# GpSimd's part of the state space preparation held until the first cross attention ends, with its zero blocks written once

## The chip, the core and the metric

The kernel runs on one core of one Trainium2 chip. The metric is device time in microseconds (us) of one launch. The core has five engines that each work through a queue of their own in order: TensorE (PE, with its weight loads shown apart as PEld), VectorE (DVE), ScalarE (ACT), GpSimd (POOL) and SyncE (SP, which here only issues transfers). They meet through semaphores, and an engine whose next instruction waits does nothing behind it either.

## What is computed

Two networks follow each other on 256 rows of 1024 numbers, in float32. The first has two layers, each a hybrid mixer followed by a cross attention to a memory of 256 rows. The second has, in layer 0, a feed-forward block, a state space mixer and a second feed-forward block, and in layer 1 the same with a sparse attention in the middle.

```python
for l in range(2):                                  # first_block
    h = h + hybrid_mixer(rms_norm(h, ...), ...)
    h = h + memory_cross_attention(rms_norm(h, ...), mem, ...)
h = rms_norm(h, norm_final)
h = h + 0.5 * swiglu(rmsnorm(h), ...)               # second_block, layer 0: "ffa0"
h = h + s5_mixer(rmsnorm(h), a, log_dt, b, c, ...)  # "mx20"
...
```

The state space mixer needs matrices that depend on its parameters alone: the discretised input matrices `bb_re`, `bb_im`, powers of the diagonal, and products of these with `b` and `c`. The kernel works them out while the first network runs, in eight tiles of eight groups, and stores them in HBM (`stash`), from where the mixer loads them at about 646 us.

## The kernel before

**The main work.** A weight block arrives from HBM as `raw` (halves of 128 x 1024), ACT copies each half to `hi` (line 156) and DVE forms the rest `lo` (line 157). TensorE multiplies in three products per block (`xh,hi`, `xh,lo`, `xl,hi`, or the like, all issued at line 72). There are three `hi` and two `lo` buffers, so DVE can be one block or so ahead of TensorE.

**Side work.** `Net.bg` is called after most groups of matmuls. It keeps an account: `share` times the modelled time of the matmuls issued is owed to a generator `self.side`, and it advances the generator until the debt is paid by the modelled time of the GpSimd instructions that came out (at least 1000 ns a step). A step that yields a true value ends the call. `share` is 0.4 in the first network and 0.7 in the feed-forward blocks.

**The preparation.** `s5_prep` joins `self.side` at the end of the first mixer. It first computes small parameters on DVE and ACT (`prm`, `pw`, `E`), then on GpSimd `bb` (six products, all GpSimd instructions are recorded at line 60), then the eight tiles of `s5_prep_tile`. A tile does, in GpSimd's order: the zeroing of `pcb` and of `pX` twice, the products that fill the two `pX`, the zeroing of a record buffer `pv` (128 x 1024), four products from `pcb` and four sums into `pv`, two stores (`stash<-pv`, the first of this record, the second of one that ACT filled at line 1302), the zeroing of the next `pv` (128 x 512, twice 128 x 4), eighteen small products, and a third store. In between ACT writes `pcb` from PSUM (lines 1279 and 1280), TensorE transposes the two `pX` and multiplies them with `pcb` (PSUM tag `pq`), and DVE copies blocks into the zeroed `pv` (line 1329). `pv` has two buffers, `pcb` and the two `pX` one each.

GpSimd keeps the order in which it is called (`InOrder`). The other engines' queues are put in order by the framework's scheduler when the program is built, and are fixed from then on. GpSimd also computes the reciprocal roots of the norms (`rq`, `rx`, `rf`), which the main work needs.

**Deadline.** `s5_inputs(2)`, called when the third quarter of ffa0's output is done, runs what is left of the generator.

Of the kernel before, what the change touches and what calls it, by code (L numbers as in the profile page):

```python
# [78 lines left out]
class Net:  # L79
    def __init__(self, ctx, tc, T):  # L80
        self.tc, self.nc, self.T = tc, tc.nc, T
        self.G, self.PE = InOrder(tc), Products(tc)
        self.at, self.owed, self.share = 0, 0, 0.4
        pool = lambda name, bufs, **kw: ctx.enter_context(tc.tile_pool(name=name, bufs=bufs, **kw))
        self.cp = pool("consts", 1)
        self.wp = pool("weights", 3)
        self.wk = pool("work", 2)
        self.sm = pool("small", 2)
        self.dr = pool("dram", 1, space=bass.MemoryType.DRAM)
        self.pp = pool("psum", 3, space=PSUM)  # L90
        self.side = iter(())

    def bg(self):

# [752 lines left out]
    def cross(self, l):  # L847
        nc, T = self.nc, self.T
        V, A, PE = nc.vector, nc.scalar, self.PE
        b1 = self.b1  # L850
        mv = self.t("qT", [P, 6, S], pool=b1).rearrange("p a b -> p (a b)")[:, :1024].rearrange("p (t c) -> p t c", t=2)
        x = self.xhat(self.hT, self.gain("norm_xattn", KD * l, KD))

        def mem_v(i):

            p = self.rows2(self.wcols(T["mem_wv"][l], 256 * i, 256), self.xmem)
            for t in range(2):
                A.activation(mv[:, t, 256 * i:256 * i + 256], p[:, t, :], AF.Copy, scale=self.rm[:, t:t + 1])
            self.bg()
            if i == 1 and l == 0:  # L860
                self.mem = self.mem_in(1)
                self.side = chain(self.mem, self.side)

        qT, kT, pr, xs = [], self.mkT, {}, []

        def queries(hp):
            p = self.proj2(self.wcols(T["mem_wq"][l], hp * 256, 256), x)
            q = self.pair(f"L{hp}", pool=b1)
            A.activation(q, p, AF.Copy)
            qT.append(q)  # L870
            self.bg()

        def scores(h):
            p2 = self.ps("pb").rearrange("p (t k) -> p t k", t=2)
            st = self.c("ast", 8, bufs=4)
            s = self.pair(f"sg{h}", pool=b1) if h < 3 else self.t("keT", [P, 512], pool=b1).rearrange("p (i s) -> p i s", i=2)
            for t in range(2):
                p = p2[:, t, :]
                PE.matmul(p, qT[h // 2][:, h % 2, t * P:(t + 1) * P], kT[:, h, :], start=True, stop=True)
            V.tensor_reduce(st[:, 0:2], p2, axis=AX.X, op=MAX)  # L880
            for t in range(2):
                V.tensor_scalar(st[:, 2 + t:3 + t], st[:, t:t + 1], rs_[:, t:t + 1], -1.0, op0=MUL, op1=MUL)
                A.activation(s[:, t, :], p2[:, t, :], AF.Exp, bias=st[:, 2 + t:3 + t], scale=rs_[:, t:t + 1],
                             accum_out=st[:, 4 + t:5 + t])
            V.reciprocal(st[:, 6:8], st[:, 4:6])
            for t in range(2):
                V.tensor_scalar(s[:, t, :], s[:, t, :], st[:, 6 + t:7 + t], None, op0=MUL)
            pr[h] = s

        def values(h):  # L890
            pt = self.ps("pb").rearrange("p (i s) -> p i s", i=2)
            for kt in range(2):
                for t in range(2):
                    PE.transpose(pt[:, kt, t * P:(t + 1) * P], pr[h][:, t, kt * P:(kt + 1) * P], self.ident)
            sT = self.pair("e2", bufs=3)
            A.activation(sT, pt, AF.Copy)
            po = self.ps("po")[:, :S]
            for kt in range(2):
                PE.matmul(po, mv[:, kt, h * P:(h + 1) * P], sT[:, kt, :], start=kt == 0, stop=kt == 1)
            hl = self.pair(f"L{2 + h}", F32R, pool=b1)  # L900
            hl = [hl[:, 0, :], hl[:, 1, :]]
            A.activation(hl[0], po, AF.Copy)  # L902
            V.tensor_tensor(hl[1], po, hl[0].bitcast(F32), op=SUB)
            xs.append(hl)

        mem_v(0)
        queries(0)
        r = self.rpow(self.sumsq(self.hT, KD, "pb"), D, 2, "rx")
        rs_ = self.c("rxs", 2)
        V.tensor_scalar(rs_, r, 1.0 / math.sqrt(128.0), None, op0=MUL)  # L910
        queries(1)
        scores(0)
        scores(1)
        scores(2)
        mem_v(1)
        values(0)
        scores(3)
        values(1)

        ws = [self.wcols(T["mem_wo"][l], c0, 512, nk=4) for c0 in (0, 512)]  # L920
        add = self.add_h()
        bank = {}

        def part(m2, ks):
            if m2 not in bank:
                bank[m2] = self.ps().rearrange("p (i s) -> p i s", i=2)
            for k in ks:
                for i in range(2):
                    c = (2 * (m2 % 2) + i) * P
                    self.mm3(bank[m2][:, i, :], [w_[:, k, c:c + P] for w_ in ws[m2 // 2]], xs[k], k + i == 0, k == 3,  # L930
                             skip_group_check=True)

        part(0, (0, 1))
        values(2)
        part(1, (0, 1))
        values(3)
        part(2, (0, 1))
        for m2 in range(4):
            part(m2, (2, 3) if m2 < 3 else range(4))
            add(m2, bank[m2])  # L940
            self.bg()

    def first_block(self):
        nc, T = self.nc, self.T
# [186 lines left out]
    def s5_prep(self):  # L1131
# [63 lines left out]
        for k in range(6):  # L1195
# [3 lines left out]
            if k == 3:  # L1199
# [17 lines left out]
        TT(v["zi"], v["zi"], v["dt"], MUL)  # L1217
        yield

        bb = self.pz.tile([P, 2, 512], F32, name="bb", tag="bb", bufs=1)  # L1220
        GT = lambda o, a, b, op: G.tensor_tensor(o, a, b, op=op)
        zb = [v[n][:, :, None].to_broadcast([P, H, 16]) for n in ("zr", "zi")]
# [2 lines left out]
        cmul([h16(bb[:, i, :]) for i in range(2)], [h16(t) for t in bn], zb,  # L1225
             [h16(s_) for s_ in sc], GT)
        yield
        for kt in range(KD):
            yield from self.s5_prep_tile(kt, v, pw, bb, E)

    def s5_c(self, kt):

# [5 lines left out]
                                       self.T[n][0, 8 * kt:8 * kt + 8].rearrange("g h p -> (g h) p")[:, None, :].to_broadcast([P, 2, 64]))  # L1238
                self.raws.append(raw)

    def s5_prep_tile(self, kt, v, pw, bb, E):
        nc, T = self.nc, self.T
        V, A, G, PE = nc.vector, nc.scalar, self.G, self.PE
        dst = self.stash[kt]
# [5 lines left out]
        v4 = lambda t: t.rearrange("p (q i c) -> p q i c", q=4, i=4)  # L1250
        half = (slice(0, 64), slice(64, 128))
        raws = self.raws
        cb = self.pt("pcb", 1).rearrange("p (a q g h) -> p a q g h", a=4, q=4, g=2)
        G.memset(cb[:, 0:2], 0.0)
        yield

        b4 = [bb[:, i, q0 * 16:(q0 + 4) * 16].rearrange("p (q h) -> p q h", h=16)[:, :, None, :].to_broadcast(qih)
              for i in range(2)]
        p4 = [pw[:, i, 0:4, q0:q0 + 4].rearrange("p j q -> p q j")[:, :, ::-1, None].to_broadcast(qih) for i in range(2)]
        sc = self.pt().rearrange("p (a q i h) -> p a q i h", a=2, q=4, i=4)  # L1260
        X = []
        for c in range(2):
            x = self.pt(f"pX{c}", 1)
            G.memset(x, 0.0)
            GT(sc[:, 0], b4[0], p4[c], MUL)
            GT(sc[:, 1], b4[1], p4[1 - c], MUL)
            yield
            for g in range(2):
                GT(v4(x)[half[g], :, :, 16 * g:16 * g + 16], sc[half[g], 0], sc[half[g], 1], ADD if c else SUB)
            X.append(x)  # L1270
            yield

        for c in range(2):
# [695 lines left out]
    def second_block(self, out):  # L1969
        scope = lambda n: self.tc.tile_pool(name=n, bufs=1)  # L1970
        at = ("ffa0", "mx20", "ffb0", "ffa1", "mx21", "ffb1")
        with ExitStack() as win, ExitStack() as keep, ExitStack() as tmp:
            self.win = win.enter_context(scope("win"))
            for i, n in enumerate(at):
                l = i // 3
                if n.startswith("ff"):
                    self.share = 0.7
                    with scope(n) as self.gp:
                        if n == "ffb1":
                            self.side = self.residual_rows()  # L1980
                        self.ffn("ffn1" if n[2] == "a" else "ffn2", l, pre=self.final_norm() if n == "ffa0" else None,
                                 out=out if n == "ffb1" else None, then=self.s5_inputs if n == "ffa0" else None,
                                 tail=self.s5_tail if n == "ffa0" else None,
                                 rb=self.rbk if n == "ffa1" else None)
                    if n == "ffb0":
                        self.ns = keep.enter_context(scope("nsakv"))
                        self.nt = tmp.enter_context(scope("nsatmp"))
                        self.shared_kv()
                elif n == "mx20":
                    drain(self.side)  # L1990
                    with scope("s5") as self.s5p:
                        self.s5()
                    win.close()
                    self.prep.close()
                else:
                    drain(self.side)
                    tmp.close()
                    with scope("nsa") as self.nq:
                        self.nsa()
                    keep.close()  # L2000
                if self.stop == n:
                    drain(self.side)
                    if n != "ffb1":
                        self.store(out)
                    return
# [104 lines left out]
```

## Time and profile before

| what | value |
|---|---|
| median of 3 runs | 1480.52 us (1480.0 to 1486.8) |
| profiled execution | 1478.54 us, its span 1476.8 us |
| PE busy | 1417.0 us (96%) |
| PEld busy | 1324.5 us (90%) |
| DVE busy | 1004.5 us (68%) |
| ACT busy | 748.1 us (51%) |
| POOL busy | 297.2 us (20%), 421 instructions |
| DMA | 252.77 MB, 171 GB/s |

The span runs from the first to the last instruction of the profiled execution; the 1.7 us around it are start and end. Busy shares are means over the whole span: POOL's 20% is made of stretches where it works all the time and others where it does nothing.

### The profile page before, as it was taken

Reading aid. Unit: us, or ns where it says so; the run is one execution under the profiler, and the core shown is the slowest. Engines: PE = TensorE matmul, PEld = TensorE weight load, DVE = VectorE, ACT = ScalarE, POOL = GpSimd, SP = SyncE. Lnnn points to the kernel's source line nnn. Section 1 sums busy time; section 2 is a strip of 40 time slices with the busy share of each in tenths; the row PEclk is TensorE's granted clock in tenths of the full one; section 3 lists DMA queues with packets and bytes.
Section 4 is the critical chain, followed back from the end, with each engine's and each line's share of the span. In section 5 each row is a group of like instructions: output and inputs, shape, how many; then the busy total and the mean of one; then the engine's idle time right before and its main releaser. Section 6 shows DMA issues by size and latency. Waiting matters only on the chain.

```text
span 1476.8 us, 29027 instructions
## 1 busy us (share of the span) xinstructions
PE 1417.0 (96%) x11787; PEld 1324.5 (90%) x11787; DVE 1004.5 (68%) x1785; ACT 748.1 (51%) x1284; POOL 297.2 (20%) x421
## 2 busy tenths in 40 slices
PE   8999969999999999998999999999999979999998
PEld 6898958888988899997899999899999967899987
DVE  6767946887758887648866765576664478657654
ACT  6745555655465454532354444454444387654432
POOL 3000061752536888700000000001000010000000
PEclk9999989999999999999999999999999989999999
DMA  6653633454654666678456655658656541256653
GB/s 189 163 158 101 198 116 102 147 165 129 204 159 131 216 220 192 212 271 285 159 170 191 186 183 185 202 158 193 195 181 197 171 143 30 80 168 184 196 184 132
DMA packets 244582, 252.77 MB, mean 171 GB/s; under 512 B 31409, under 2 KB 226839, under 8 KB 243680
## 3 DMA queue, kind: packets, MB, share of 16 engines
q1 hardware_dynamic: 239696, 236.20, 52.0%
q0 software_dynamic: 4464, 14.63, 3.1%
q8 instruction: 93, 1.52, 0.4%
q14 instruction: 41, 0.34, 0.1%
q10 hardware_dynamic: 288, 0.07, 0.0%
HBM read 235.40 MB, written 15.47 MB: 170 GB/s over the span
## 4 chain that ended last, share of the span: by engine, by line
PE 42%; issue 8%; DVE 2%; POOL 1%; ACT 0%; DMA 0%; POOLq 0%; DVEq 0%; ACTq 0%
PE ps L72 39%; PE pb L72 2%; PE pq L72 1%; DVE lo L157 0%; POOL hq L60 0%; DMA raw<-in_w_o_dram 0%; DVE rab L1553 0%; PE po L72 0%; DVE rz L1552 0%; DVE hqm L1624 0%; DVE lo L251 0%; DVE s L1889 0%; ACT hi L156 0%; POOL rff L60 0%; ACT o L1803 0%
## 5 line engine op out<-in xcount | busy, mean ns | idle before, releaser
L156 ACT ACTIVATE hi<-raw 128x1024 fp32r<-128x1024 f32 (+4 forms) x420 | 421.1, 1011 | 490.0 <-PE ps L72 194.7
L157 DVE TENSOR_TENSOR lo<-raw,hi 128x1024 fp32r<-128x1024 f32 (+4 forms) x420 | 496.6, 1198 | 106.1 <-issue 54.5
L72 PE MATMUL ps<-xh,hi 128*128 128x256 f32 x1848 | 524.6, 284 | 1.0 <-ACT xh L404 0.6
L72 PE MATMUL ps<-xh,lo 128*128 128x256 f32 x1848 | 521.2, 282 | 3.5 <-DVE lo L157 3.5
L72 PE MATMUL ps<-xl,hi 128*128 128x256 f32 x1848 | 521.3, 282 | 0.1
L72 PEld LDWEIGHTS ps<-xh,hi 128*128 128x128 f32 x1848 | 349.9, 189 | 9.3 <-issue 5.9
L72 PEld LDWEIGHTS ps<-xh,lo 128*128 128x128 f32 x1848 | 349.7, 189 | 5.7 <-DVE lo L157 4.1
L72 PEld LDWEIGHTS ps<-xl,hi 128*128 128x128 f32 x1848 | 349.9, 189 | 3.7 <-issue 2.5
L72 PE MATMUL ps<-gl,hi 128*128 128x256 f32 x576 | 163.5, 284 | 2.9 <-DVE gl L1570 2.9
L72 PE MATMUL ps<-gh,hi 128*128 128x256 f32 x576 | 162.9, 283 | 0.4 <-ACT gh L1569 0.4
L72 PE MATMUL ps<-gh,lo 128*128 128x256 f32 x576 | 162.5, 282 | 0.0
L72 PEld LDWEIGHTS ps<-gl,hi 128*128 128x128 f32 x576 | 109.5, 190 | 4.1 <-DVE gl L1570 3.3
L72 PEld LDWEIGHTS ps<-gh,hi 128*128 128x128 f32 x576 | 109.2, 190 | 2.1 <-issue 1.0
L72 PEld LDWEIGHTS ps<-gh,lo 128*128 128x128 f32 x576 | 109.5, 190 | 0.4 <-issue 0.2
L1056 DVE TENSOR_TENSOR ab<-ps,rbf 128x512 f32<-128x512 f32 x66 | 45.5, 690 | 67.9 <-PE ps L72 62.6
L72 PE MATMUL ps<-L,hi 128*128 128x256 f32 (+1 forms) x384 | 72.9, 286 | 0.8 <-ACT L L902 0.7
L72 PEld LDWEIGHTS ps<-L,hi 128*128 128x128 f32 (+1 forms) x384 | 58.3, 182 | 2.0 <-ACT L L902 1.5
L72 PE MATMUL ps<-L,lo 128*128 128x256 f32 (+1 forms) x192 | 54.2, 284 | 1.4 <-DVE bc L747 1.4
L251 DVE TENSOR_TENSOR gl<-e,gh 128x512 fp32r<-128x512 f32 x44 | 33.3, 758 | 30.8 <-ACT gh L250 30.8
L60 POOL TENSOR_TENSOR rkvs<-rkvsa,mhalf 128x2 f32<-128x2 f32 x1 | 0.7, 696 | 190.1 <-DVE rkvsa L384 190.1
L1062 DVE SCALAR_TENSOR_TENSOR e<-e,ab 128x512 f32<-128x512 f32 x44 | 33.6, 764 | 6.9 <-ACT e L1061 6.7
L72 PEld LDWEIGHTS ps<-L,lo 128*128 128x128 f32 (+1 forms) x192 | 35.0, 183 | 2.2 <-DVE bc L747 1.7
(578 smaller groups left out, 2376.1 us busy)
## 6 DMA issues: line engine op xcount, KB each, us to landing
raw<-in_ffn_w_in_dram SPq DMA_DIRECT2D x176, 512.0 KB, 4.2
raw<-in_ffn_w_out_dram SPq DMA_DIRECT2D x68, 512.0 KB, 4.3
raw<-in_w_in_dram SPq DMA_DIRECT2D x24, 512.0 KB, 6.6
stash<-pv POOLq DMA_DIRECT2D x24, 512.0 KB, 3.9
raw<-in_ffn_w_out_dram SPq DMA_DIRECT2D x24, 384.0 KB, 3.4
raw<-in_w_out_dram SPq DMA_DIRECT2D x16, 512.0 KB, 4.1
raw<-in_w_in_dram SPq DMA_DIRECT2D x24, 256.0 KB, 3.7
rec<-stash SPq DMA_DIRECT2D x4, 1536.0 KB, 8.8
```

Of the source, the lines that this page charges most:

```text
L60: return self.tc.keep_in_program_order(f(out, *a, **k))
L72: return self.engine.matmul(out, w, x, **k)
L156: self.nc.scalar.activation(dst(h), src(raw), AF.Copy)
L157: (engine or self.nc.vector).tensor_tensor(dst(l), src(raw), dst(h).bitcast(F32), op=SUB)
L251: self.nc.vector.tensor_tensor(lo, src, hi.bitcast(F32), op=SUB)
L1056: V.tensor_tensor(v[-1], p, rb2, op=MUL)
L1062: V.scalar_tensor_tensor(th, th, 1.0, v[0], op0=ADD, op1=MUL)
```

## The change

`self.hold` starts as true and is cleared when `cross` returns for the first time. In `s5_prep` the part on GpSimd, from `bb` on, is preceded by a loop that yields true while the flag is up, so that each `bg` stops there. The zeroing of `pcb` and of the two `pX` moves out of the tile into `s5_prep`, ahead of the loop over tiles, and all eight tiles write the same three buffers. What stands between the blocks that are filled stays zero. `share` is 0.8 in ffa0 and 0.7 in the other feed-forward blocks.

```diff
@@ Net.__init__
+        self.hold = True
@@ cross, at its end
             self.bg()
+        self.hold = False
@@ s5_prep
+        while self.hold:
+            yield True
         bb = self.pz.tile([P, 2, 512], F32, name="bb", tag="bb", bufs=1)
...
         yield
+
+        cb = self.pt("pcb", 1).rearrange("p (a q g h) -> p a q g h", a=4, q=4, g=2)
+        G.memset(cb[:, 0:2], 0.0)
+        X = [self.pt(f"pX{c}", 1) for c in range(2)]
+        for x in X:
+            G.memset(x, 0.0)
+        yield
         for kt in range(KD):
-            yield from self.s5_prep_tile(kt, v, pw, bb, E)
+            yield from self.s5_prep_tile(kt, v, pw, bb, E, cb, X)
@@ s5_prep_tile
-        cb = self.pt("pcb", 1).rearrange("p (a q g h) -> p a q g h", a=4, q=4, g=2)
-        G.memset(cb[:, 0:2], 0.0)
-        yield
...
-        X = []
-        for c in range(2):
-            x = self.pt(f"pX{c}", 1)
-            G.memset(x, 0.0)
+        for c, x in enumerate(X):
             GT(sc[:, 0], b4[0], p4[c], MUL)
             GT(sc[:, 1], b4[1], p4[1 - c], MUL)
             yield
             for g in range(2):
                 GT(v4(x)[half[g], :, :, 16 * g:16 * g + 16], sc[half[g], 0], sc[half[g], 1], ADD if c else SUB)
-            X.append(x)
             yield
@@ second_block
-                    self.share = 0.7
+                    self.share = 0.8 if n == "ffa0" else 0.7
```

The built order shows what the scheduler makes of this. First GpSimd's queue at the first cross attention, whose norm is `rx`; before, `bb` and the first tile stand here.

```order
L60 TENSOR_TENSOR bb<-pX_1679,prm 128x512
L60 TENSOR_TENSOR pv<-pX_1680,prm 128x512
L60 TENSOR_TENSOR bb<-pX_1679,prm 128x512
L60 TENSOR_TENSOR pv<-pX_1680,prm 128x512
L60 TENSOR_TENSOR bb<-bb,pv 128x512 x2
L60 MEMSET pcb 128x256
L60 MEMSET pX_1931 128x512
L60 TENSOR_TENSOR pt<-bb,pw 128x256 x2
L60 TENSOR_TENSOR pX_1931<-pt 64x16x16 x2
L60 MEMSET pX_2057 128x512
L60 TENSOR_TENSOR pt<-bb,pw 128x256 x2
```

In the change GpSimd passes from `rx` to the second mixer's small work (`on`, `keT`, `r`, `rkv`, `rq`), and `bb` follows behind `rq`.

```order
L60 TENSOR_TENSOR rx<-rxa,mhalf 128x2
L60 MEMSET on_2677 16x256
L60 DMA on_2677<-in_gla_w_gate_dram 16x4x48
L60 MEMSET keT 128x512
L60 MEMSET keT 128x8
L60 TENSOR_TENSOR r_2774<-r1a,mhalf 128x2
L60 TENSOR_TENSOR rkv<-rkva,mhalf 128x2
L60 TENSOR_TENSOR rq<-rqa,mhalf 128x2
L60 TENSOR_TENSOR bb<-pX_1679,prm 128x512
L60 TENSOR_TENSOR pv<-pX_1680,prm 128x512
L60 TENSOR_TENSOR bb<-pX_1679,prm 128x512
```

The `bb` products and tile 0 moved from ahead of `rx` to behind the second mixer's `rq`.

Next ACT's queue at the first tile's `pcb` (the last two of its eight copies). Before, it stands in the first cross attention, with the queries' copy, the squares for the norm (`sq<-hT`) and a weight block behind it.

```order
L1279 ACTIVATE pcb<-pq 64x4x16
L1280 ACTIVATE pcb<-pq 64x4x16
L869 ACTIVATE L_2277<-ps 128x512
L365 ACTIVATE sq<-hT 128x512 x2
L156 ACTIVATE hi<-raw 128x1024
L373 ACTIVATE sq<-pb 128x256
L156 ACTIVATE hi<-raw 128x1024 x2
```

In the change it stands in the second mixer, ahead of the weights for the queries and of the exponentials of the gates (`ei`, `eb`, `ek`).

```order
L1283 ACTIVATE pcb<-pq 64x4x16
L1284 ACTIVATE pcb<-pq 64x4x16
L157 ACTIVATE hi<-raw 128x6x96
L555 ACT_TABLE_LOAD
L555 ACTIVATE ei<-bc 128x512
L557 ACTIVATE eb<-bc 128x512
L556 ACTIVATE ek<-ek 128x512
```

So the same eight copies, which need the zeroed `pcb`, moved from ahead of the norm's squares to ahead of the gates' exponentials.

Last DVE's queue in ffa0 around the copies into `pv` of tile 6. Before, they are followed by the rest of a gate and by the weight blocks of the next matmuls.

```order
L1056 TENSOR_TENSOR ab<-ps,rbf 128x512
L157 TENSOR_TENSOR lo<-raw,hi 128x1024
L1323 SCALAR_TENSOR_TENSOR pt<-ident,prm,pq 32x32 x4
L1329 COPY pv<-pt 32x4x32 x2
L1329 COPY pv<-pt 64x4x32
L1329 COPY pv<-pt 32x4x32 x2
L1329 COPY pv<-pt 128x4x32
L1062 SCALAR_TENSOR_TENSOR e_6880<-e_6880,ab 128x512
L157 TENSOR_TENSOR lo<-raw,hi 128x1024
L1056 TENSOR_TENSOR ab<-ps,rbf 128x512
L157 TENSOR_TENSOR lo<-raw,hi 128x1024
L1063 TENSOR_TENSOR e_6880<-e_6880,ab 128x512
```

In the change:

```order
L158 TENSOR_TENSOR lo<-raw,hi 128x1024 x2
L1064 SCALAR_TENSOR_TENSOR e_6847<-e_6847,ab 128x512
L1327 SCALAR_TENSOR_TENSOR pt<-ident,prm,pq 32x32 x4
L1333 COPY pv<-pt 32x4x32 x2
L1333 COPY pv<-pt 64x4x32
L1333 COPY pv<-pt 32x4x32 x2
L1333 COPY pv<-pt 128x4x32
L1058 TENSOR_TENSOR ab<-ps,rbf 128x512
L158 TENSOR_TENSOR lo<-raw,hi 128x1024
L1065 TENSOR_TENSOR e_6847<-e_6847,ab 128x512
L158 TENSOR_TENSOR lo<-raw,hi 128x1024
L252 TENSOR_TENSOR gl_6852<-e_6847,gh_6851 128x512
```

(`ab` is a scaled product, `e` the gate that is being formed, `gl` its rest.) The neighbours are of the same kind; what moved is the distance from tile to tile. Counted in TensorE instructions that stand between the copies of one tile and those of the next, it was 349, 302 and 403 before (tiles 4 to 7; 3221, 3570, 3872 and 4275 in TensorE's list), and is 256, 262, 256 and 257 in the change (tiles 3 to 7; 3106, 3362, 3624, 3880 and 4137).

## Rows read from the trace of the kernel before

**Rows 1.** What TensorE waited for, 180 to 224 us: total, times, longest (us)
```profile
PE pb L72 <- ACT sq L365: 7.9, 1, 7.9
```

**Rows 2.** Timeline of ACT in the first cross attention: start, duration, instruction
```profile
190.22 0.22 ACT L1279 ACTIVATE pcb<-pq 64x64 f32<-64x64 f32 x1 [8.02 <-POOL pcb L60]
```

**Rows 3.** Timeline of GpSimd at the same place
```profile
181.02 1.07 POOL L60 TENSOR_TENSOR bb<-pX,prm 128x512 f32<-128x512 f32 x1 [49.91 <-DVE prm L1161]
...
189.88 0.31 POOL L60 MEMSET pcb<- 128x256 f32 x1
```

**Rows 4.** Timeline of DVE: additions into hT that bound both cross attentions
```profile
172.32 0.67 DVE L244 TENSOR_TENSOR hT<-ps,hT 128x512 f32<-128x512 f32 x1
...
228.41 0.69 DVE L244 TENSOR_TENSOR hT<-ps,hT 128x512 f32<-128x512 f32 x1 [0.95 <-PE ps L72]
...
399.73 0.69 DVE L244 TENSOR_TENSOR hT<-ps,hT 128x512 f32<-128x512 f32 x1 [0.56 <-PE ps L72]
...
443.58 0.69 DVE L244 TENSOR_TENSOR hT<-ps,hT 128x512 f32<-128x512 f32 x1 [1.18 <-PE ps L72]
```

**Rows 5.** Timeline of GpSimd in the first feed-forward
```profile
462.91 0.69 POOL L60 TENSOR_TENSOR rf<-rfc,mhalf 128x2 f32<-128x2 f32 x1
...
470.30 0.53 POOL L60 MEMSET pX<- 128x512 f32 x1
...
476.05 0.95 POOL L60 MEMSET pv<- 128x1024 f32 x1
...
490.30 0.61 POOL L60 MEMSET pv<- 128x512 f32 x3 [2.61 <-DMA stash<-pv]
...
530.17 0.61 POOL L60 MEMSET pv<- 128x512 f32 x3 [2.04 <-DMA stash<-pv]
...
571.37 0.61 POOL L60 MEMSET pv<- 128x512 f32 x3 [2.48 <-DMA stash<-pv]
...
586.62 0.60 POOL L60 DMA_DIRECT2D stash<-pv  x1 [0.30 <-POOL pv L60]
...
616.01 0.53 POOL L60 DMA_DIRECT2D stash<-pv  x1 [6.70 <-ACT pr L1312]
616.58 0.60 POOL L60 MEMSET pv<- 128x512 f32 x3
...
627.51 0.59 POOL L60 DMA_DIRECT2D stash<-pv  x1 [0.30 <-POOL pv L60]
```

**Rows 6.** What DVE waited for, 466 to 629 us
```profile
DVE pv L1329 <- POOL pv L60: 4.9, 2, 3.3
```

**Rows 7.** Timeline of TensorE in the first feed-forward
```profile
480.20 1.03 PE L76 MATMUL pq<-ident,pX 128*128 128x128 f32 x8
...
575.12 0.38 PE L72 MATMUL ps<-xh,lo 128*128 128x256 f32 x1 [1.58 <-DVE lo L157]
...
610.50 1.04 PE L76 MATMUL pq<-ident,pX 128*128 128x128 f32 x8
```

**Rows 8.** What TensorE waited for, 466 to 629 us
```profile
PE pq L72 <- ACT pv L1302: 5.5, 3, 3.0
```

**Rows 9.** Groups of GpSimd by form: busy us, mean ns, idle before
```profile
L60 POOL MEMSET pX<- 128x512 f32 x16 | 8.6, 535 | 0.5
...
L60 POOL MEMSET pcb<- 128x256 f32 x8 | 2.6, 328 | 0.0
```

**Rows 10.** Timeline of GpSimd in the second mixer
```profile
260.29 0.92 POOL L60 TENSOR_TENSOR rq<-rqa,mhalf 128x2 f32<-128x2 f32 x1 [3.14 <-DVE rqa L384]
```

**Rows 11.** Timeline of ACT in the second mixer
```profile
266.83 1.93 ACT L156 ACTIVATE hi<-raw 128x768 fp32r<-128x768 f32 x4
```

**Rows 12.** GpSimd's instructions, 466 to 629 us: ns minimum/median/maximum, first and last start
```profile
L60 POOL TENSOR_TENSOR pt<-bb,pw x16: 646/1040/1670, 467.2 to 594.0; 128x256 f32<-128x256 f32 x16
...
L60 POOL TENSOR_TENSOR pv<-pt x16: 732/1226/1624, 478.5 to 606.8; 64x256 f32<-64x256 f32 x16
```

**Rows 13.** Busy us (and count) of PE, PEld, DVE, ACT, POOL; PEclk, DMA
```profile
490.00:611.00 121.00, 118.69 (x1031) 117.61 (x1031) 95.42 (x112) 57.85 (x90) 102.05 (x131) 1.00 0.65 207
```

More of the change, by code (lines that the diff above doesn't have):

```diff
@@ L1239, in s5_c, with s5_prep_tile @@
                 self.raws.append(raw)
-    def s5_prep_tile(self, kt, v, pw, bb, E):
+    def s5_prep_tile(self, kt, v, pw, bb, E, cb, X):
         nc, T = self.nc, self.T
```

## The prediction

> **What bounds the kernel now.** I read four things in order. First, the page: TensorE is busy for 96% of the span, so the change can only win in the few places where TensorE waits, and can lose wherever it makes a new wait. Second, the waits of TensorE in the first cross attention. One stands out: 7.9 us for the norm's squares on ACT [rows 1]. ACT's timeline says why: ACT sat for 8.02 us in front of the eight copies into `pcb`, which need GpSimd's zeroing of `pcb` [rows 2], and the squares stand behind those copies in ACT's queue. GpSimd's timeline shows the cause: the six products of `bb` come first, from 181.02 to the zeroing at 189.88, 8.9 us [rows 3]. Third, the same stage twice: from the mixer's last addition into `hT` to the cross attention's first it is 56.1 us in layer 0 and 43.9 us in layer 1, at 300 TensorE instructions each in the built order [rows 4]. Fourth, the first feed-forward, where four of the eight tiles are made. GpSimd reaches the second zeroing of a tile (the `pv` of 128 x 512) at 490.30, 530.17, 571.37 and 616.58 [rows 5]: 39.9, 41.2 and 45.2 us apart, the last with 6.7 us of waiting for ACT. It works there without pause. DVE already waits for it, 4.9 us in two waits [rows 6], and TensorE, by way of DVE, 1.58 us at 575.12 [rows 7]; three more waits of TensorE at the tiles' own products make 5.5 us [rows 8].
>
> **Part 1: the first cross attention loses its stall.** GpSimd has nothing but `rx` to do there, and the `pcb` copies are gone from ACT's queue. If the stage then takes what its twin in layer 1 takes, the gain is 56.1 - 43.9 = 12.2 us [rows 4]; the twin carries side work of a tile as well, so I see no reason for less than the bare wait of 7.9 us [rows 1]. I take -12.2, bounds -7.9 and -13.
>
> **Part 2: the second mixer gets it.** The `bb` products now start when `rq` is done, before at 260.29 + 0.92 = 261.2 us [rows 10]. They took 8.9 us [rows 3], so `pcb` is zeroed at about 270.1 on that clock, later if DVE, which is busy there, holds them up. ACT, in its queue, gets to the copies behind the 768-wide weight block that ended at 268.8 [rows 11]. So ACT waits again, for 1.3 us or more, with weights and the gates' exponentials behind it, and DVE and then TensorE behind those. Nearest row for the upper end: the whole old wait, 7.9 us [rows 1]. I take +3, nearer to the lower end because ACT comes later here; bounds 0 and 7.9.
>
> **Part 3: the zeroing.** A zeroing of `pX` takes 0.535 us, one of `pcb` 0.328 us [rows 9]. Per tile 2 x 0.535 + 0.328 = 1.4 us of GpSimd go, seven times. This has a value only where GpSimd is late, which is part 4.
>
> **Part 4: the first feed-forward, closer tiles.** This is the term that decides. In TensorE's list the copies of DVE into `pv` stood 349, 302 and 403 instructions apart and now stand about 258 apart. One TensorE instruction here takes 118.69 / 1031 = 0.115 us [rows 13], so TensorE now asks for a tile every 29.7 us. Before, GpSimd took 39.9, 41.2 and 45.2 - 6.7 = 38.5 us for a tile of its own accord [rows 5], 39.9 in the mean, and 39.9 - 1.4 = 38.5 without the zeroing. DVE cannot pass its copies, which need the second zeroing, and in the change the block whose `lo` stands behind them is needed some 70 TensorE instructions later (copies at 3106, 3362, 3880 and 4137, block at 3176, 3435, 3953 and 4212). So GpSimd would set TensorE's pace from the first of these copies to the last.
>
> How fast GpSimd is then depends on DVE. A product into `pt` took 0.646 us at least and 1.040 in the median, a sum into `pv` 0.732 and 1.226 [rows 12]; the two kinds for `pX` and from `pcb` are like them. Four of each kind per tile make 16 instructions and 4 x 2 x (0.394 + 0.494) = 7.1 us over their minimum. The eighteen small products show it too: from the second zeroing to the third store it took 586.62 - 571.37 = 15.3 us in tile 6 and 627.51 - 616.58 = 10.9 us in tile 7 [rows 5], 4.3 us more. Together 11.4 us of a tile are delay. I estimate that the delay goes with the DVE work that passes in a tile, and thus with its TensorE instructions: 258 now, and before 39.9 x 1031 / 121 = 340 [rows 13]. That leaves 11.4 x 258 / 340 = 8.7 us, and 38.5 - 2.7 = 35.8, say 36 us a tile. Bounds: 38.5 (the delay stays as it is) and 27.1 (it all goes, as DVE stands still while it waits for GpSimd).
>
> The Trainium skill has a rule for this ("SBUF — State Buffer", section "Who interferes with whom"): a DVE instruction with two inputs in SBUF shares a port with a GpSimd instruction that reads SBUF, not with one that only writes, and the later one waits for the whole instruction. The trace agrees so far: the zeroing of `pX`, which only writes, has a mean of 535 ns beside products that stretch from 646 to 1670 [rows 9, 12]. By the rule a blocked DVE delays nothing, which speaks for the lower bound; it is a rival below.
>
> Now the clock of the stage. Zero is the end of `rf`, before at 463.6 [rows 5]. In the change the second half of tile 3 follows it: half of the `pX` work (476.05 - 470.30 - 0.53 = 5.2 us) and what lies between the two zeroings (490.30 - 476.05 = 14.3), so the first zeroing that DVE waits for is at 483.1. Four tiles of 36 us later, tile 7's is at 627.1. At 575.12 TensorE went on 3.75 us behind the zeroing at 571.37 [rows 5, 7]; so here at 630.9, with the block at 4212. Before, it was at 4229 at 610.50 [rows 7], so at 4212 at 608.5; the change has 13 more TensorE instructions between `rf` (3030 in the list, before 3043) and there, 1.5 us. The loss is 630.9 - 610.0 = 20.9 us, less the last of the old waits [rows 8], which came later (5.5 / 3 = 1.8 us is the mean of the three): **+19**. With 38.5 us a tile it is +29. With 27.1 TensorE paces again: only tile 3's late start is left: its copies at 3106 hold up the product at 3176, which before ran at 480.20 [rows 7], so 483.1 + 3.75 - (480.20 + 1.5) = 5 us, and the old waits of 5.5 and 1.6 us go: -2.
>
> The meter's 0.8 has no other cost: it changes where side work stands, and that is counted. Tile 7's copies stand 138 instructions (16 us) earlier in TensorE's list than before, so its stores stay ahead of the loads of `stash` at least as far as they were. The drain in `s5_inputs` finds an empty generator.
>
> **Sum.** Against the profiled execution: 1478.5 - 12.2 + 3 + 19 = 1488.3 us. The median of the runs shown lies 2.0 us above that execution, so 1490 us.
>
> **Rivals.**
> (a) GpSimd keeps the old delay: 38.5 us a tile. For it: DVE has the same work to catch up after each wait, so GpSimd's first products meet a full DVE. Time: 1490 + 10 = 1500.
> (b) The delay vanishes when DVE stands still, and TensorE paces itself: 1478.5 - 12.2 + 3 - 2 + 2 = 1469, faster. It decides from 33.5 us a tile downwards (there part 4 costs 9 us and the change is even); 31.7 would make it faster by 0.5%. For it: the minima of the products [rows 12]. The port rule of the Trainium skill that is cited above points the same way. Against it: DVE stands still while GpSimd waits for its own store or makes the last sums of a tile, not while it does the eighteen products.
> (c) The old wait comes back whole in the second mixer (7.9 instead of 3) and part 4 goes as in (b): 1474, no change to speak of.
> That the hold does nothing is ruled out: `bb` stands behind `rq` in the built order.
>
> **Chances.** My forecast 0.50, (a) 0.15, (b) 0.20, (c) 0.15. A measurement of this kernel can tell about 0.5%, 7.4 us. Slower by more than that: 0.40 of the forecast's 0.50 (its own range is 1481 to 1498), and (a): 0.55. Within: the rest of the forecast and most of (c): 0.24. Faster: (b) and a little: 0.21. The range from 1466 to 1506 leaves some 0.1 below and 0.08 above.
>
> **What would show it.** In the profile of the change: no wait of ACT for `pcb` and none of TensorE for `sq` in the first cross attention, with some 44 us between its two additions; a shorter wait of ACT for `pcb` at about 255 us; in ffa0 the second zeroings 35 to 37 us apart, each with a wait of DVE behind it (`pv` for `pv`) of several us, and TensorE waiting for `lo` or for the `pX`. If the zeroings come every 30 us and TensorE shows no such waits, part 4 is wrong; if the stage in the first cross attention stays above 50 us, part 1 is.

## The result, and the profile after

The changed kernel takes 1499.72 us (median of four runs, 1498.9 to 1501.57), the kernel before 1483.66 us beside it (1480.0 to 1487.64). The ratio is 1.0104 with a 95% interval of 1.0082 to 1.0127: **slower by 1.04%, which is 15.4 us**. The forecast was 1490 us, range 1466 to 1506, slower with a chance of 0.55.

The waits of TensorE from 180 to 224 us, as in [rows 1] (waited for, total, times, longest, us), no longer hold the 7.9 us for `sq`:

```profile
PE pb L72 <- ACT sq L366: 1.2, 1, 1.2
PE pb L76 <- DVE xl L406: 0.9, 1, 0.9
PE ps L72 <- ACT L L903: 0.6, 1, 0.6
```

DVE's additions into `hT` (start, duration), to be read against [rows 4]: the first cross attention now lies between 172.95 and 215.41, 42.5 us against 56.1.

```profile
172.95 0.68 DVE L245 TENSOR_TENSOR hT<-ps,hT 128x512 f32<-128x512 f32 x1
215.41 0.69 DVE L245 TENSOR_TENSOR hT<-ps,hT 128x512 f32<-128x512 f32 x1 [1.18 <-PE ps L72]
...
393.73 0.69 DVE L245 TENSOR_TENSOR hT<-ps,hT 128x512 f32<-128x512 f32 x1 [1.88 <-PE ps L72]
438.44 0.69 DVE L245 TENSOR_TENSOR hT<-ps,hT 128x512 f32<-128x512 f32 x1 [1.17 <-PE ps L72]
...
680.66 0.42 DVE L1086 SCALAR_TENSOR_TENSOR hT<-ps,hT 128x256 f32<-128x256 f32 x1 [2.70 <-PE ps L72]
```

The second mixer, from 215.41 to 393.73, takes 178.3 us (before 228.41 to 399.73, 171.3). TensorE's timeline there has two waits in a row, in the products beside the gates:

```profile
264.55 0.34 PE L72 MATMUL ps<-L,lo 128*64 128x256 f32 x1 [3.76 <-DVE lo L158]
...
267.00 0.47 PE L72 MATMUL ps<-L,lo 128*64 128x256 f32 x1 [1.53 <-DVE bc L748]
```

In the first feed-forward GpSimd's timeline gives the second zeroings of the five tiles, the counterpart of [rows 5], 36.9, 36.0, 36.3 and 35.8 us apart:

```profile
473.68 0.60 POOL L60 MEMSET pv<- 128x512 f32 x3 [1.85 <-DMA stash<-pv]
...
510.59 0.61 POOL L60 MEMSET pv<- 128x512 f32 x3 [1.87 <-DMA stash<-pv]
...
546.62 0.61 POOL L60 MEMSET pv<- 128x512 f32 x3 [1.84 <-DMA stash<-pv]
...
582.89 0.60 POOL L60 MEMSET pv<- 128x512 f32 x3 [1.91 <-DMA stash<-pv]
...
618.69 0.60 POOL L60 MEMSET pv<- 128x512 f32 x3 [1.85 <-DMA stash<-pv]
```

DVE stands in front of each of them (DVE's timeline, the first one; and DVE's waits from 440 to 660 us, against [rows 6]), and TensorE in front of DVE (TensorE's waits there, against [rows 7, 8]):

```profile
474.24 1.39 DVE L1333 COPY pv<-pt 32x128 f32<-32x128 f32 x6 [2.73 <-POOL pv L60]
```

```profile
DVE pv L1333 <- POOL pv L60: 13.6, 5, 2.8
```

```profile
PE ps L72 <- DVE lo L158: 13.6, 6, 4.3
PE pq L76 <- POOL pX L60: 7.6, 3, 3.2
```

A window (us, then busy time and count of PE, PEld, DVE, ACT, POOL, then TensorE's granted clock and DMA) shows what came with the waits; 1.00 is 2.4 GHz, 0.50 is 1.2 GHz, and a value between is a stretch with both. Before, the window of [rows 13] stood at 1.00.

```profile
470.00:500.00 30.00, 25.55 (x196) 25.15 (x194) 23.31 (x33) 13.51 (x24) 24.66 (x35) 0.89 0.59 191
500.00:530.00 30.00, 27.30 (x229) 26.90 (x230) 20.73 (x30) 13.06 (x25) 24.64 (x36) 0.94 0.62 199
```

The profiled execution has a span of 1497.7 us, 20.9 more than before. Of these 16.8 are there at the end of the first feed-forward (680.66 against 663.82) and 15.8 still at 941.50 (before 925.70). The other 5 us of the 20.9 lie behind that, in stages that the change doesn't touch; the ratio of the runs (15.4 us) doesn't show them.

### The profile page after: what moved, and what is told of

Same layout as the page of the kernel before. It is cut to its first block, busy times and chain, and to the rows that moved or that the text cites. A ratio compares the mean times of both kernels' runs of the same rounds, so it can differ in the third digit from the quotient of the medians.

```text
span 1497.7 us, 29016 instructions
## 1 busy us (share of the span) xinstructions
PE 1434.5 (96%) x11787; PEld 1341.4 (90%) x11787; DVE 994.9 (66%) x1785; ACT 747.6 (50%) x1284; POOL 278.9 (19%) x400
## 4 chain that ended last, share of the span: by engine, by line
PE 42%; issue 8%; DVE 2%; POOL 1%; ACT 0%; DMA 0%; POOLq 0%; DVEq 0%; ACTq 0%
PE ps L72 39%; PE pb L72 2%; PE pq L72 1%; DVE lo L158 0%; POOL hq L60 0%; DMA raw<-in_w_o_dram 0%; DVE rab L1557 0%; PE po L72 0%; DVE rz L1556 0%; DVE hqm L1628 0%; DVE lo L252 0%; DVE s L1893 0%; ACT hi L157 0%; POOL rff L60 0%; ACT o L1807 0%
```

## The experiments

Three stages are read in every trace from the additions into `hT`. C1: from the first mixer's last to the first cross attention's first. M2: from there to the second mixer's last. F: from the second cross attention's last to the last of ffa0. The second cross attention itself, between M2 and F, takes 49.9 to 51.8 us in every trace but that of e11 (63.9). In us:

| kernel | C1 | M2 | F | ratio to before (95%) |
|---|---|---|---|---|
| before | 56.1 | 171.3 | 213.7 | |
| the change | 42.5 | 178.3 | 236.2 | 1.0104 (1.0082 to 1.0127) |
| e1 meter 0.7 | 42.6 | 176.8 | 221.5 | 0.9986 (0.9967 to 1.0004) |
| e2 no hold | 56.2 | 173.5 | 230.4 | 1.0107 (1.0075 to 1.0139) |
| e3 hold alone | 43.6 | 174.9 | 229.3 | 1.0044 (1.0021 to 1.0067) |
| e4 zero-once alone | 55.2 | 173.7 | 222.1 | 1.0055 (1.0039 to 1.0071) |
| e5 no hold, `pcb` early, 0.6 | 57.1 | 173.6 | 214.2 | 1.0008 (0.9991 to 1.0024) |
| e6 as e1, `pcb` early | 42.6 | 176.9 | 223.1 | 1.0013 (0.9990 to 1.0036) |
| e7 as e1, no `bb` | 44.0 | 172.8 | 224.4 | 0.9995 (0.9972 to 1.0019) |
| e8 no small products | 42.0 | 176.9 | 217.2 | 0.9974 (0.9957 to 0.9991) |
| e9 as e1, later hold | 42.4 | 177.6 | 222.0 | 1.0014 (1.0001 to 1.0027) |
| e10 as the change, 0.5 / 0.6 | 42.4 | 184.8 | 217.0 | 1.0041 (1.0024 to 1.0057) |
| e11 as e9, 0.6 / 0.5 | 44.1 | 189.9 | 204.6 | 1.0026 (1.0014 to 1.0037) |
| e12 as e9, `pcb` early | 44.2 | 173.5 | 221.1 | 0.9978 (0.9957 to 0.9998) |

**The parts apart.** e1, the meter back:

```diff
-                    self.share = 0.8 if n == "ffa0" else 0.7
+                    self.share = 0.7
```

> The change with the meter of the first feed-forward back at 0.7; hold and zero-once stay. The copies of DVE into pv then stand at 3148, 3413, 3714, 4021 and 4398 of TensorE's list, 1250 instructions from first to last (143.8 us at 0.115 us each), where GpSimd needs 4 x 36 = 144 us. Theory (GpSimd's 36 us a tile against the 29.7 us that the meter of 0.8 asks for): only the late first tile is left, some 5 us of the 23.1 that ffa0 lost; time 1478 to 1488 us, below before or even. Rival (the loss in ffa0 comes from the hold, which leaves five tiles to this stage, whatever the meter): 1495 to 1500, as the change.

1482.61 us, as the theory said. F is 14.7 us shorter than in the change; 7.9 more than before are left. e2, the hold out:

```diff
-        while self.hold:
-            yield True
```

> The change without the hold; zero-once and 0.8 stay. The work starts in the first cross attention again, so the wait for pcb there comes back and the 7.0 us of the second mixer go: 0 against before up to ffa0. The copies into pv that fall behind rf stand at 3119, 3378, 3637 and 3896, again 258 apart. Theory: DVE waits for each of these zeroings, which come 36 us apart; the first some 8 us late, the three after it 6.3 us each later, less the 7 us of old waits: +20, 1500 to 1508. Rival (the hold does it): 1478 to 1486, and no wait of DVE of 2 us or more for the zeroing.

1502.38 us: the size is that of the theory, and the way is another. The zeroings come 37.8, 36.4 and 37.5 us apart, at 480.91, 518.66, 555.07 and 592.61, but DVE hardly waits for them (1.5 us in two waits). TensorE's waits in ffa0 show that it now meets GpSimd at its own transposes of `pX`:

```profile
PE pq L76 <- POOL pX L60: 16.5, 6, 4.5
```

e3 is before with the hold alone, e4 the change without the hold and with 0.7:

```diff
e3 (to before)
+        self.hold = True
...
+        self.hold = False
...
+        while self.hold:
+            yield True
e4 (to the change)
-        while self.hold:
-            yield True
...
-                    self.share = 0.8 if n == "ffa0" else 0.7
+                    self.share = 0.7
```

> Before with the hold alone: zeroing per tile, meter 0.7. The copies behind rf stand at 3202, 3551, 3858, 4253 and 4554, 338 apart in the mean (38.9 us), where GpSimd needs 38.5. Theory: first cross attention -13.6, second mixer +7.0, ffa0 about +3 for the tile more: 1478 to 1485. Rival (the hold does it): 1495 or more.

1491.65 us (1485.31 to 1496.16): neither expected value. The mistake was to count only how far apart the tiles stand. The last one is asked for so late that its rest falls into the end of the stage. GpSimd's timeline shows it held there by its own store, and TensorE's what that costs, by way of the copies for the decay (line 1372) that stand behind it in DVE's queue:

```profile
656.92 0.60 POOL L60 MEMSET pv<- 128x512 f32 x3 [6.34 <-DMA stash<-pv]
```

```profile
668.16 0.58 PE L72 MATMUL ps<-gh,hi 128*128 128x256 f32 x1 [5.22 <-DVE hT L1086]
```

> Before with the zero-once alone: no hold, meter 0.7. GpSimd's list has 1.4 us less a tile, but the meter counts the same zeroing less and so puts the tiles closer: copies at 3122, 3426, 3688 and 3996 behind rf, 304, 262 and 308 apart (35.0, 30.1, 35.4 us), GpSimd 36. Theory: the first some 8 us late, then 1.0 + 5.9 + 0.6 more, less 7 us of old waits: +8, 1488 to 1496. Rival (less work for GpSimd can only help): 1478 to 1484.

1493.29 us, as the theory said: an edit that only takes work from GpSimd makes the kernel slower by 0.55%, since the meter no longer counts the work that is gone, and so asks for the next tile sooner. DVE's waits in ffa0:

```profile
DVE pv L1331 <- POOL pv L60: 9.1, 4, 2.8
```

**Is it GpSimd's pace?** e8 is the change with the eighteen products left out and only counted by the meter:

```diff
-        G.memset(fr[:, 0, :, 0:1], 1.0)
-        G.memset(fr[:, 1, :, 0:1], 0.0)
+        ns = G.ns
+        G.memset(fr, 0.0)
+        G.ns = ns + 7.2
...
         for k in range(6):
             n = 1 << k
+            G.ns += 3 * 2.6 * 8 * n
...
-            GT(new, new, tm[:, :, :, 0:n], ADD)
```

> The change with GpSimd's eighteen small products of each tile left out (half of the third record is zeroed instead); the meter counts them all the same, so that the tiles stand where the change has them, 258 TensorE instructions apart. Theory (GpSimd's 36 us a tile is what paces ffa0): without the 9 to 11 us of these products it needs some 26 us, less than the 29.7 asked; the second zeroings come 30 to 31 us apart, DVE's waits for them are gone, and of ffa0's 23 us loss 0 to 5 are left: 1476 to 1485. Rival (the copies' place in DVE's queue and the tile's own chain over ACT and TensorE cost the time, whatever GpSimd has to do): 1493 or more.

1478.16 us. With the tiles at the same places, GpSimd's second zeroings are now 29.6, 30.5, 33.0 and 30.8 us apart, and F is 217.2 us: 3.5 of the 22.6 us are left. Together with e1, where the same work is asked for less often, this shows GpSimd's pace as the cause. It doesn't show what share of it is the length of the eighteen products and what share is their effect on DVE, since both go with them.

```profile
472.35 0.99 POOL L60 MEMSET pv<- 128x512 f32 x2 [1.84 <-DMA stash<-pv]
501.95 0.99 POOL L60 MEMSET pv<- 128x512 f32 x2 [1.42 <-DMA stash<-pv]
532.49 0.99 POOL L60 MEMSET pv<- 128x512 f32 x2
565.53 0.99 POOL L60 MEMSET pv<- 128x512 f32 x2 [0.99 <-DMA stash<-pv]
596.31 0.99 POOL L60 MEMSET pv<- 128x512 f32 x2 [1.67 <-DMA stash<-pv]
```

**Where the second mixer's 7 us come from.** e6 zeroes `pcb` ahead of `bb`, e7 keeps GpSimd about as busy (7.56 us against 9.2) with nothing that reads; both have the meter at 0.7:

```diff
e6
+        cb = self.pt("pcb", 1).rearrange("p (a q g h) -> p a q g h", a=4, q=4, g=2)
+        G.memset(cb[:, 0:2], 0.0)
         bb = self.pz.tile([P, 2, 512], F32, name="bb", tag="bb", bufs=1)
...
-        cb = self.pt("pcb", 1).rearrange("p (a q g h) -> p a q g h", a=4, q=4, g=2)
-        G.memset(cb[:, 0:2], 0.0)
e7
...
-        cmul([h16(bb[:, i, :]) for i in range(2)], [h16(t) for t in bn], zb,
-             [h16(s_) for s_ in sc], GT)
...
+        for k in range(16):
+            G.memset(bb[:, k % 2, :], 0.0)
...
```

> As the run with hold, zero-once and meter 0.7, but pcb is zeroed ahead of the products of bb. It tells apart two causes of the second mixer's loss (from the cross attention's first addition to the mixer's last 178.3 us in the change, 171.3 before). Theory A, as in the prediction: ACT's 1.7 us wait for pcb and what stands behind it; then the stage falls to 171 to 174 and the time to 1477 to 1480. Theory B: the products of bb stretch DVE's two-input instructions beside them (lo of 128x1024 took 1.68 us there, 1.21 before), and TensorE's wait of 3.8 us for lo follows from that; then the stage stays at 176 to 178 and the time at 1481 to 1484, with no wait of ACT for pcb.

> As the run with hold, zero-once and meter 0.7, but bb isn't computed: sixteen zeroings of 128x512, 0.535 us each, stand in the place of its six products, so that GpSimd is busy as long but reads nothing. Theory B (GpSimd's reading products stretch DVE): lo of 128x1024 takes 1.2 us in the gates' stretch of the second mixer, TensorE's wait of 3.8 us for lo is gone or under 1 us, the stage takes 171 to 174 us and the whole 1477 to 1480. Theory A (ACT's wait for pcb): the wait of ACT stays, the stage 176 to 178, the whole 1481 to 1484.

e6: 1483.59 us, M2 stays at 176.9, and TensorE still waits 4.58 us for `lo`. e7: M2 falls to 172.8, and that wait to 1.45 us. The timelines of DVE, of before, the change and e7 in this order, show why: the same `lo` of 128x1024 takes 1.21, 1.68 and 1.22 us.

```profile
262.55 1.21 DVE L157 TENSOR_TENSOR lo<-raw,hi 128x1024 fp32r<-128x1024 f32 x1
264.07 1.24 DVE L157 TENSOR_TENSOR lo<-raw,hi 128x1024 fp32r<-128x1024 f32 x1
```

```profile
250.95 1.68 DVE L158 TENSOR_TENSOR lo<-raw,hi 128x1024 fp32r<-128x1024 f32 x1
252.95 1.69 DVE L158 TENSOR_TENSOR lo<-raw,hi 128x1024 fp32r<-128x1024 f32 x1
254.56 1.78 DVE L252 TENSOR_TENSOR L<-L,L 128x512 fp32r<-128x512 f32 x1
```

```profile
250.29 1.22 DVE L158 TENSOR_TENSOR lo<-raw,hi 128x1024 fp32r<-128x1024 f32 x1
251.81 1.22 DVE L158 TENSOR_TENSOR lo<-raw,hi 128x1024 fp32r<-128x1024 f32 x1
252.94 0.69 DVE L252 TENSOR_TENSOR L<-L,L 128x512 fp32r<-128x512 f32 x1
```

In e7 ACT doesn't wait for `pcb` either, since its copies stand behind the exponential `ei` there; e6 shows that this alone changes nothing. So theory B holds for the stage. Its whole time (1482.12) didn't fall with it: F is 2.9 us longer than in e1, since GpSimd's five zeroings there span 156.0 us (470.17 to 626.17) against 150.3 (472.20 to 622.49), and GpSimd's pace took back what the mixer gave. Why its tiles took longer there is open.

**Looking for a better place.** e5 drops the hold and takes the zeroing of `pcb` ahead of `bb` as e6 does, with 0.6 in ffa0:

```diff
-        while self.hold:
-            yield True
...
-                    self.share = 0.8 if n == "ffa0" else 0.7
+                    self.share = 0.6 if n == "ffa0" else 0.7
```

> A version made from what the first four runs showed: no hold, the zero blocks written once, the zeroing of pcb ahead of the products of bb instead of behind them, meter 0.6 in ffa0. The copies into pv behind rf then stand at 3167, 3477, 3829 and 4268, 310, 352 and 439 apart (35.7, 40.5 and 50.5 us), GpSimd 36. Theory: ACT no longer waits 8 us for pcb in the first cross attention, so TensorE loses the 7.9 us wait there (-8 to -13.6); nothing of the preparation's start falls into the second mixer; ffa0 costs 0 to 3. Time 1468 to 1478. Rival (the stall is only moved, since the products of bb slow DVE wherever they stand): 1480 to 1490.

1483.72 us, a miss, within the rival's range: F is cured (214.2), C1 isn't. TensorE's waits in the first cross attention are no longer one of 7.9 us but these, with `bb` and the first tile still in that stage:

```profile
PE pb L72 <- ACT sg L884: 3.9, 1, 3.9
PE pq L76 <- POOL pX L60: 3.7, 2, 2.2
PE pb L72 <- ACT sq L366: 1.4, 1, 1.4
```

e9 ends the hold behind the gates of the second mixer (meter 0.7):

```diff
         V.tensor_tensor(ek, gk, ek, op=MUL)
+        if l:
+            self.hold, self.share = False, 0.4
+            g = self.c("gated", 2)
+            self.G.tensor_tensor(g, ek[:, 0, 0:2], ek[:, 1, 0:2], op=MUL)
...
-        self.hold = False
...
-                    self.share = 0.8 if n == "ffa0" else 0.7
+                    self.share = 0.7 if n == "ffa0" else 0.7
```

> As the run with hold, zero-once and meter 0.7, but the hold ends behind the second mixer's gates, not at the end of the first cross attention: a GpSimd product of two columns of ek, which the gates' last product writes, stands ahead of bb's products, so that these start some 17 us later. Theory B (reading products of GpSimd stretch DVE, and the gates are where DVE has no slack): no wait of TensorE of over 1 us for lo in the gates, the second mixer (first addition of the cross attention to its own last) 172 to 174 us against 176.8, the whole 1477 to 1481. Rival (these products cost the same wherever they stand): 176 to 178 and 1482 to 1485.

1485.6 us, a miss: the wait for `lo` is down to 0.4 us, but ACT now stands 5.27 us in front of the zeroing of `pcb`, with `kT` behind it, and TensorE (below) waits for that.

```profile
268.06 0.22 ACT L1286 ACTIVATE pcb<-pq 64x64 f32<-64x64 f32 x1 [5.27 <-POOL pcb L60]
269.51 0.59 ACT L589 ACTIVATE kT<-ps 64x512 f32<-64x512 f32 x1
```

```profile
270.15 1.01 PE L72 MATMUL ps<-hi,L 128*128 128x384 f32 x2 [5.93 <-ACT kT L589]
```

e10 and e11 try faster tiles between the hold and ffa0, so that ffa0 has fewer:

```diff
e10 (to the change)
         self.hold = False
+        self.share = 0.5
...
-                    self.share = 0.8 if n == "ffa0" else 0.7
+                    self.share = 0.6 if n == "ffa0" else 0.7
e11 (to e9)
-            self.hold, self.share = False, 0.4
+            self.hold, self.share = False, 0.6
...
-                    self.share = 0.7 if n == "ffa0" else 0.7
+                    self.share = 0.5 if n == "ffa0" else 0.7
```

> The change with the meter at 0.5 from the end of the hold to the end of the first network (0.4 before), and 0.6 in ffa0. The copies into pv then stand at 1892, 2201, 2631, 2922 ahead of rf and at 3263, 3573, 3925, 4275 behind it: four tiles in ffa0 as before the change, 310 to 352 apart (35.7 to 40.5 us) where GpSimd needs 36. Theory: first cross attention -13.6, second mixer +7.0, ffa0 0 to +3: 1474 to 1481, faster than before. Rival (the loss moves to where the tiles now are closer, 1892 to 2201 in the second mixer): 1483 to 1490.

> The hold that ends behind the gates, the meter at 0.6 from there to the end of the first network and at 0.5 in ffa0: copies at 1940, 2194, 2494, 2798 ahead of rf and at 3105, 3469, 3872, 4275 behind it, 364 to 403 apart in ffa0 (42 to 46 us). Theory: first cross attention -13.6, second mixer +1.5 to +3, ffa0 0 or below (its old waits of 7 us go in part), closer tiles in the second cross attention 0 to +3: 1468 to 1477, the fastest of all. Rival (GpSimd sets the pace in the second mixer and cross attention instead, at 254 to 304 instructions a tile): 1480 to 1490.

1488.99 and 1489.01 us: the rivals were right. F is 217.0 and 204.6 us, in e11 9 less than before, but M2 is 184.8 and 189.9. In e11 the second cross attention grows as well, from 50.4 to 63.9 us (407.97 to 471.92). The mixer needs a small GpSimd result itself, `rg`, and it stands in GpSimd's queue behind the tile. DVE's wait in e10 and TensorE's behind it:

```profile
DVE on L717 <- POOL rg L60: 6.3, 1, 6.3
```

```profile
PE pb L76 <- DVE on L717: 5.6, 2, 5.0
```

The wait for `lo` in the gates is there in e10 too (5.4 us). In e11's second cross attention TensorE waits for GpSimd's `pX` (408 to 472 us); the rest of the 13.5 us there was not traced:

```profile
PE pq L76 <- POOL pX L60: 6.3, 2, 4.5
```

e12 is e9 with the zeroing of `pcb` ahead of the hold:

```diff
+        cb = self.pt("pcb", 1).rearrange("p (a q g h) -> p a q g h", a=4, q=4, g=2)
+        G.memset(cb[:, 0:2], 0.0)
         while self.hold:
             yield True
...
-        cb = self.pt("pcb", 1).rearrange("p (a q g h) -> p a q g h", a=4, q=4, g=2)
-        G.memset(cb[:, 0:2], 0.0)
```

> As e9 (hold to the end of the second mixer's gates, zero-once, meter 0.7), but pcb is zeroed before the hold, so that ACT's copies into it, which now stand at 1357 of TensorE's list, wait for nothing. In e9 TensorE waited 5.9 us for kT, which stands in ACT's queue behind those copies. Theory (the second mixer's loss has two sources, DVE stretched by the products of bb, and ACT held by the zeroing behind them; each run so far took away one): neither wait of TensorE is left (lo in the gates and kT each under 1.5 us), the second mixer takes 171 to 174 us against 176.8 and 177.6, and the time is 1478 to 1482. Rival (a third cause in the second mixer): 175 us or more.

1480.25 us, ratio 0.9978 (0.9957 to 0.9998): M2 is 173.5, the wait for `kT` is 1.9 us (1.5 at most was expected) and that for `lo` 0.4. Of the versions that leave nothing out it has the lowest ratio, 0.2% below before. Whether it is faster than e1 isn't shown: e1's 0.9986 (0.9967 to 1.0004) overlaps it.

## Why the forecast came out, step by step

**Part 1** held: -13.6 us (56.1 to 42.5) against -12.2 forecast, 0.6 beyond the bound of -13. The twin that it was taken from carries a tile's products of TensorE, and this stage now carries none. e2, e4 and e5, without the hold, all keep 55 to 57 us, and e3, the hold alone, has 43.6, so the hold is what does it.

**Part 2 was mis-sized**: 7.0 us against +3, still under the bound of 7.9, and the path was another. The prediction let the loss start at ACT's wait for `pcb`. That wait is there, 1.72 us at 257.79, but e6 takes it away and M2 stays. The step that failed is the clause "later if DVE, which is busy there, holds them up": it asks only what DVE does to GpSimd. In the gates it is GpSimd that holds up DVE, whose instructions follow each other there without a gap. TensorE waits 3.76 us for `lo`. Windows of the gates and of the whole of M2, the change's first in each pair, show the clock beside it:

```profile
247.00:277.00 30.00, 24.71 (x163) 23.87 (x163) 25.59 (x30) 19.02 (x39) 27.56 (x28) 0.83 0.28 79
260.00:290.00 30.00, 27.48 (x197) 25.90 (x197) 25.73 (x36) 21.70 (x43) 25.32 (x28) 0.94 0.43 125
215.41:393.73 178.32, 167.84 (x1282) 155.57 (x1281) 133.25 (x234) 95.40 (x182) 75.25 (x104) 0.96 0.49 146
228.41:399.73 171.32, 163.23 (x1284) 150.69 (x1283) 130.57 (x235) 95.66 (x182) 69.54 (x102) 0.99 0.50 152
```

Read in steps of 1 us, the clock is at 0.50 in both kernels for some 3 us ahead of the gates' last products (249 to 252 in the change, 261 to 264 before), and in the change once more right behind the waits of 3.76 and 1.53 us, from 266 to 272. That is 0.11 x 30 = 3.3 us more, of which some 0.5 fall into the second wait.

Over the whole of M2 waiting is the smaller part: TensorE stands idle for 178.3 - 167.8 = 10.5 us against 8.1 before, 2.4 more, since other waits got shorter. The remaining 4.6 of the 7.0 us are time at the lower clock, and about 1.8 of them a third stretch, 358 to 361, some 90 us behind the gates. e1, whose edit begins in ffa0, doesn't have that one, and its M2 is 1.5 us shorter; so some 5.5 of the 7.0 us are the gates' part.

The rule of the Trainium skill that the prediction used in part 4 ("SBUF — State Buffer", section "Who interferes with whom") has this side too: whichever of the two comes second is blocked. e7 agrees: beside zeroings, which only write, `lo` takes 1.22 us, beside reading products 1.68. Without those products M2 still has 1.5 us over before.

**Part 3** has the wrong sign where it stands alone (e4). The prediction gave it a value only where GpSimd is late; that the meter takes the saved time back, by asking sooner, is part of the 258 instructions of part 4, but was not said.

**Part 4** held and was a little small: 22.6 us (213.7 to 236.2) against +19. Its steps, one by one: a tile takes 36.25 us ((618.69 - 473.68) / 4; forecast 36); the first awaited zeroing is 16.4 us behind the end of `rf` at 457.32 (forecast 19.5); TensorE goes on 3.9 us behind a zeroing (586.81 behind 582.89; forecast 3.75), and behind the first and the last 5.1 and 4.7. It reaches the block behind the last copies 166.1 us after `rf` (623.41; forecast 167.3).

The 36 came out in total, less so in its parts. The estimate shortened the eighteen products as well, but from the second zeroing to the third store GpSimd takes 14.3, 15.2, 15.2 and 15.2 us in tiles 3 to 6, as before (14.1, 16.0 and 15.3 in tiles 4 to 6); what got shorter are products such as the sums into `pv`, 0.737 us in the median against 1.226.

What the sum didn't have is the clock: 0.89 to 0.96 in the windows from 470 to 640, in all 0.11 x 30 + 0.06 x 60 + 0.04 x 80 = 10.1 us of full speed; before, 450 to 510 had 0.94 and the rest 1.00, 3.6 us. TensorE's waits grow from 9.2 to 22.1 us. That is 12.9 + 6.5 = 19.4 of the 22.6. Most of the last 3 us is no wait but work: with five tiles in this stage instead of four TensorE makes 134 of their products (`pq`) where it made 108. The 108 took 9.8 us, so a fifth tile is about 2.5.

The sum of the stages is -13.6 + 7.0 + 22.6 = 16.0, beside the forecast's 9.8. The errors of parts 2 and 4 have one sign: each prices waits and leaves out the time at the lower clock. Of the 9.7 us between 1490 and 1499.72 the errors of parts 1, 2 and 4 make 6.2; 3.1 more come from the kernel before, which has a median of 1483.66 here and 1480.52 in the runs that the forecast started from. The direction was right with a chance of only 0.55, and the time lies above the 1481 to 1498 that the prediction gave its own forecast.

**Rivals.** (a), 38.5 us a tile, is out by the zeroings, 36.25 us apart, although its time of 1500 us is the one that was measured: the number alone would have pointed at the wrong cause. (b), TensorE sets the pace, is out in the change. e8 shows that its condition was the right one: at 31.0 us a tile in the mean, F is 3.5 us over before and the kernel is faster. (c) is out with it, though its 7.9 us in the second mixer were nearer than my 3.

What stays open: e12 still takes 7.4 us more than before in ffa0, with five tiles there instead of four (some 2.5 us of it the fifth tile's own products). A version with e12's second mixer and four tiles in ffa0 wasn't tried; e10 and e11 show that the missing tile can't come from the second mixer at this price.

## What to carry to other kernels

A meter that asks for side work by a modelled time has to be held against what that engine really takes per unit: here a tile was asked for every 29.7 us and took 36, and taking 1.4 us of work out of each tile with the meter's share unchanged (e4) cost 0.55%. Before moving reading GpSimd work, look for the stretch where DVE has no gap, and for small results of GpSimd or writes of ACT that will stand behind it: each of three places tried for `bb` had another victim (`sq` on ACT, `lo` on DVE, `kT` on ACT). Price the clock beside the waits: in the second mixer 4.6 of the 7.0 us lost were time at the lower clock, and in ffa0 some 6 of the 22.6.

## What the runs showed of the hardware that I had not expected

A DVE instruction with two inputs in SBUF can more than double beside reading GpSimd products: `L<-L,L` of 128x512 took 1.78 us in the change and 0.69 beside zeroings (e7). Both engines stretch: of the six products of `bb` in the change the first two took 1.06 us each, the fourth 2.04 and the last two 3.98 together. A pair of waits of 3.76 and 1.53 us, between 260.8 and 267.0 us, was followed by a granted clock of 0.50 (1.2 GHz) up to 272, where it had been 1.00 from 253 to 265.
